# The block inversion of an RWKV-7 kernel, with its levels cut to the columns that they alter

## The chip, the cores and the metric

The kernel runs on one core of one Trainium2 chip. The metric is the device time of one execution in microseconds (us), as the median of several runs; lower is better. The engines are called as in the profile: PE is TensorE's matmul and PEld its weight load, DVE is VectorE, ACT is ScalarE, POOL is GpSimd, SP is SyncE, which issues most of the DMAs.

## The reference

One decoder block on 512 tokens of 2048 channels, in float32. A first projection feeds three things: an RWKV-7 time mixer with 16 heads of 64, sliding-window attention with 16 query heads, and two sigmoid gates that merge the two branches. After the merge follows a gated feed-forward network with a short convolution, 5632 wide. The change concerns the time mixer, whose reference is a scan over tokens with one 64 x 64 state per head:

```
def step(state, inp):
    r_t, k_t, v_t, w_t, ka_t, kb_t = inp
    sa = jnp.einsum('bhvk,bhk->bhv', state, ka_t)
    state = (state * w_t[:, :, None, :] + sa[..., None] * kb_t[:, :, None, :]
             + v_t[..., None] * k_t[:, :, None, :])
    y = jnp.einsum('bhvk,bhk->bhv', state, r_t)
    return state, y
```

Every token reads the state that the tokens before it wrote. The kernel cuts the 512 tokens into 8 chunks of 64 (NCH chunks of C). What the tokens of one chunk do to each other is a triangular system of 64 x 64 per chunk and head, and inverting its matrix replaces 64 steps by a few matrix products.

## The kernel before

**The run as a whole.** Projections come first, each a product of a 2048-channel weight slice with all 512 tokens; attention follows, then the time mixer, the merge, and the feed-forward network. A float32 product is made as three products of high and low parts: `project` (L251) issues high x high (L259), high x low (L260) and low x high (L261) for each of 16 blocks of 128 channels, each a matmul of 128 x 128 by 512 columns. So one projection tile is 48 such matmuls. `load_w` (L235) fetches the weights and makes their high part on ACT (L242) and their low part on DVE (L243).

**The time mixer.** Its 16 heads go in pairs: heads on partitions 0 to 63 and 64 to 127, eight pairs `p`. For each pair `early(p)` (L601) makes the inputs, with three projection tiles for k, r and v; `late(p)` (L656) does the chunk work; `final(p)` (L783) normalises the output, with a row of factors that goes through memory and back (L384 to L388); three gate tiles of the merge follow (`emit_gate`, L365). The loop at L805 emits late(p), early(p+1), final(p), three gates. The kernel does not fix the order of the instructions here: a planner of the framework sets each engine's order when the program is built, from estimated costs and the dependencies. On PE it puts projections of early(p+1) and of the gates between the products of late(p). Each engine then works through its instructions in that order.

**The inversion.** `BX` holds, for each of the 8 chunks, a block-diagonal 128 x 128 matrix with one 64 x 64 block per head. The inverse is built by doubling: LEVELS are 1, 2, 4, 8, 16, 32; at level m the blocks of 2m columns on the diagonal are finished from the blocks of m. The right factor of the first product, `X`, is the inverse so far, stacked for both heads (128 partitions x 8 chunks x 64 columns) and held as a high and a low f16 part, `X[:, 0]` and `X[:, 1]`. `AI` is the matrix, transposed and scaled by SG = 4096, also as two f16 parts, and `BT` the transposed inverse so far. The masks `m1` to `m32` (L103) keep of a product the columns whose place within their block of 2m is m or later, with the rows of the block's first half, and the diagonal. Level 1 is the start (L691 to L707). Each of the five other levels is (L729 to L749):

1. `mm3(ps, AI, X)`: for each of 8 chunks three f16 matmuls of 64 columns (L725 to L727), accumulated in one PSUM bank `bulk` (three banks);
2. DVE multiplies by the level's mask (L734), `split` makes the f16 parts `IW` on ACT and DVE (L205, L206);
3. `mm3(ps, BT, IW)`: 24 more matmuls;
4. ACT and DVE write the two heads' blocks of `BX` from the bank (L739, L740);
5. except in the last level, ACT and DVE write `X` anew (L742, L743), PE transposes `BX` in two times four blocks (L748), and `split` makes `BT` from them.

Then a scan over the chunks (L752 to L769) uses `BX`, and L776 to L778 make the output.

Of the kernel before, what the change touches and what calls it, by code (L numbers as in the profile page):

```python
# [8 lines left out]
F32 = mybir.dt.float32  # L9
# [3 lines left out]
AF = mybir.ActivationFunctionType  # L13
ALU = mybir.AluOpType
# [4 lines left out]
P = 128  # L19
# [3 lines left out]
C = 64  # L23
NCH = S // C
# [6 lines left out]
SG = 4096.0  # L31
# [102 lines left out]
def block_kernel(ctx: ExitStack, tc: tile.TileContext, d: Dims, a: dict, out: bass.AP):  # L134
    nc = tc.nc
    act, dve, pool, pe, sync = nc.scalar, nc.vector, nc.gpsimd, nc.tensor, nc.sync
# [31 lines left out]
    xt = [p0.tile([P, d.D], F32, name=f"xi{t}") for t in range(NT)]  # L168
# [35 lines left out]
    def split(hi, lo, src, pin=free):  # L204
        pin(act.activation(hi, src, AF.Copy))  # L205
        pin(dve.tensor_tensor(lo, src, hi.bitcast(F32) if hi.dtype == F32R else hi, op=ALU.subtract))  # L206
# [75 lines left out]
    if True:  # L282
# [109 lines left out]
        with ExitStack() as pt:  # L392
# [4 lines left out]
            def small():  # L397
                return mps.tile([P, S], F32, name="mi", tag="mi")
# [25 lines left out]
            for t in range(NKV):  # L424
# [12 lines left out]
                ps = small().rearrange("p (n c) -> p n c", c=P)  # L437
# [16 lines left out]
            for g in range(NHK):  # L454
# [7 lines left out]
                for n in range(NT):  # L462
# [9 lines left out]
                    sc = ap_.tile([P, GQ, 2 * BLK], F32, name="sc", tag="sc", bufs=2)  # L472
                    pr_ = ap_.tile([P, GQ, 2 * BLK], F32, name="pr", tag="pr", bufs=2)
                    for h in range(GQ):
                        slope = float(2.0 ** (-8.0 * (g * GQ + h + 1) / d.HQ))
                        dve.scalar_tensor_tensor(sc[:, h, k0:], K["dist"][:, k0:], slope, scp[h % 2][:, h // 2, k0:],
                                                 op0=ALU.mult, op1=ALU.add)
# [15 lines left out]
                    for kb in kbs:  # L493
                        ps = small().rearrange("p (h c) -> p h c", c=P)
# [6 lines left out]
                    ps = small()[:, : GQ * HD].rearrange("p (h c) -> p h c", c=HD)  # L501
                    for h in range(GQ):
                        for kb in kbs:
                            pe.matmul(ps[:, h], pT[:, kb, h], vt[:, n - 1 + kb, g * HD : (g + 1) * HD],  # L504
                                      start=kb == kbs[0], stop=kb == kbs[-1])
                    ot = ap_.tile([P, GQ, HD], F32, name="ot", tag="ot", bufs=2)
                    dve.tensor_tensor(ot, ps, rc.unsqueeze(2).to_broadcast([P, GQ, HD]), op=ALU.mult)
                    ps = small()[:, : GQ * HD].rearrange("p (j c) -> p j c", c=P)
# [7 lines left out]
        with ExitStack() as pr:  # L516
# [3 lines left out]
            wk = pr.enter_context(tc.tile_pool(name="wk", bufs=1, reuse_waits="tile"))  # L520
# [14 lines left out]
            def wtile(tag, bufs=1):  # L535
                return wk.tile([P, S], F32, name=tag, tag=tag, bufs=bufs)

            def bulk():
                return blk.tile([P, S], F32, name="bulk", tag="bulk")
# [15 lines left out]
            for i in range(NG):  # L555
                acc = ztile(d.c_gd + i * P)
                t = wtile("lw")
# [4 lines left out]
            def bdtile(nm):  # L562
                t = bd.tile([P, NCH, P], F32, name=nm)
                pool.memset(t[0:C, :, C:P], 0.0)
                pool.memset(t[C:P, :, 0:C], 0.0)
                return t

            BX = bdtile("BX")
# [14 lines left out]
            AI = bd.tile([P, 2, NCH, P], F16, name="AI")  # L583
            BT = bd.tile([P, 2, NCH, P], F16, name="BT")
            def r3(ap, c=C):
                return ap.rearrange("p (n c) -> p n c", c=c)
# [69 lines left out]
            def late(p, st):  # L656
# [13 lines left out]


                XIW = wk.tile([P, 4, NCH, C], F16, name="XIW", tag="rhl")
                X, IW = XIW[:, 0:2], XIW[:, 2:4]
                tt = wk.tile([P, NCH, C], F32, name="tt", tag="dd")
                HN = NCH // 2

                def mb(nm, n, h=None):
                    m = K[nm] if h is None else K[nm][h[0] : h[1]]
                    return m.unsqueeze(1).to_broadcast([m.shape[0], n, m.shape[-1]])
# [3 lines left out]
                for n0 in range(0, NCH, 2):  # L683
                    ps = bulk().rearrange("p (q c) -> p q c", c=P)
# [6 lines left out]
                for g in range(2):  # L691
                    ns = slice(g * HN, (g + 1) * HN)
                    for h, (lo, hi) in enumerate(HV):
                        own = AB[lo:hi, ns, h]
                        (dve.tensor_copy if h else act.copy)(BX[lo:hi, ns, lo:hi], own)
                        dve.tensor_tensor(tt[lo:hi, ns], own, mb("m1", HN, (lo, hi)), op=ALU.mult)
                        act.copy(own, BAR[lo:hi, ns, h, 0])
                    dve.tensor_tensor(tt[:, ns], tt[:, ns], mb("istack", HN), op=ALU.add)
                    split(X[:, 0, ns], X[:, 1, ns], tt[:, ns])
                    ps = bulk().rearrange("p (n c) -> p n c", c=P)  # L700
                    for j in range(HN):
                        pe.transpose(ps[:, j], BX[:, g * HN + j], ident)
                    at_ = wk.tile([P, HN, P], F32, name="at_", tag="at_")
                    dve.scalar_tensor_tensor(at_, ps, SG, mb("idsg", HN), op0=ALU.mult, op1=ALU.add)
                    split(AI[:, 0, ns], AI[:, 1, ns], at_)
                    for i in range(2):
                        dve.tensor_tensor(BT[:, i, ns], AI[:, i, ns], mb("t1bd", HN), op=ALU.mult)  # L707
                for g in range(2):
                    ns = slice(g * HN, (g + 1) * HN)
                    ps = bulk().rearrange("p (n c) -> p n c", c=P)  # L710
# [3 lines left out]
                    ps = bulk().rearrange("p (n h c) -> p n h c", h=2, c=C)  # L714
# [4 lines left out]
                        act.copy(SV[lo:hi, ns, 1 - h], ps[lo:hi, :, 1 - h])  # L719


                def mm3(ps, wt, xt):
                    for n in range(NCH):
                        dst = r3(ps)[:, n]
                        pe.matmul(dst, wt[:, 0, n], xt[:, 0, n], start=True, stop=False)  # L725
                        pe.matmul(dst, wt[:, 0, n], xt[:, 1, n], start=False, stop=False)
                        pe.matmul(dst, wt[:, 1, n], xt[:, 0, n], start=False, stop=True)  # L727

                for m in LEVELS[1:]:  # L729
                    last = m == LEVELS[-1]  # L730
                    ps = bulk()
                    mm3(ps, AI, X)
                    tt = wk.tile([P, NCH, C], F32, name="tt", tag="dd")
                    dve.tensor_tensor(tt, r3(ps), mb(f"m{m}", NCH), op=ALU.mult)  # L734
                    split(IW[:, 0], IW[:, 1], tt)
                    ps = bulk()
                    mm3(ps, BT, IW)
                    sc = 1.0 / (SG * SG) if last else 1.0 / SG
                    act.activation(BX[0:C, :, 0:C], r3(ps)[0:C], AF.Copy, scale=sc)  # L739
                    dve.tensor_scalar(BX[C:P, :, C:P], r3(ps)[C:P], sc, None, op0=ALU.mult)  # L740
                    if not last:
                        act.activation(X[:, 0], r3(ps), AF.Copy, scale=sc)  # L742
                        dve.scalar_tensor_tensor(X[:, 1], r3(ps), sc, X[:, 0], op0=ALU.mult, op1=ALU.subtract)  # L743
                        for g in range(2):
                            ns = slice(g * HN, (g + 1) * HN)
                            ps = bulk().rearrange("p (n c) -> p n c", c=P)
                            for j in range(HN):
                                pe.transpose(ps[:, j], BX[:, g * HN + j], ident)  # L748
                            split(BT[:, 0, ns], BT[:, 1, ns], ps)  # L749


                for n in range(NCH):  # L752
                    ps = chn.tile([P, C], F32, name="psG", tag="chn")
# [4 lines left out]
                    ps = chn.tile([P, C], F32, name="psU", tag="chn")  # L758
# [5 lines left out]
                    ps = chn.tile([P, C], F32, name="psS", tag="chn")  # L764
                    for h, (lo, hi) in enumerate(HV):
                        pe.matmul(ps[lo:hi], KK[:, n, h], UV[:, n, h], start=True, stop=True)  # L766
                    for h, (lo, hi) in enumerate(HV):
                        dve.scalar_tensor_tensor(SV[lo:hi, n + 1, h], SV[lo:hi, n, h], ee[lo:hi, n : n + 1], ps[lo:hi],
                                                 op0=ALU.mult, op1=ALU.add)  # L769


                ps = bulk()
                for n in range(NCH):
                    for h, (lo, hi) in enumerate(HV):
                        dst = r3(ps)[lo:hi, n]
# [29 lines left out]
            for p in range(NP):  # L805
                lt = late(p, st)
                if p + 1 < NP:
                    st = early(p + 1)
                final(p, lt)
                for _ in range(GATES_PER_PAIR * NK // 16):  # L810
                    emit_gate()
# [71 lines left out]
    with ExitStack() as pbb:  # L883
# [9 lines left out]
        for m, i in order:  # L893
            hi, lo, r0, n, gi = parts[i]
# [11 lines left out]
            if second:  # L906
                w = min(XC, d.D)
                for e in range(m * XC, (m + 1) * XC, w):
                    t, c0 = divmod(e, d.D)
# [309 lines left out]
    with tc.tile_pool(name="sqp", bufs=1, side="right", reuse_waits="tile") as sqp:  # L1219
# [3 lines left out]
        for i in range(len(PRODUCTS)):  # L1223
            nm = PRODUCTS[i][0]
            last = i == len(PRODUCTS) - 1
# [82 lines left out]
    with ExitStack() as pd:  # L1308
        pxy = pd.enter_context(tc.tile_pool(name="psD", bufs=1, space=PSUM, reuse_waits="tile"))
        acc = {n: banks(pxy, n) for n in "XY"}  # L1310
        for i in range(len(PRODUCTS)):
            nm = PRODUCTS[i][0]
            for c in range(NB["dn"]):
                if i == 0 and c == 1:
# [7 lines left out]
                    xa = xp.tile([P, NT, d.D], F32, name="xa")  # L1322
# [81 lines left out]
```

## Time and profile before

| | |
|---|---|
| median of 3 runs | 2936.24 us (2934.93 to 2939.33) |
| the profiled execution | 2935.18 us, of which its span is 2933.4 us |
| granted PE clock, mean | 0.997 |
| DMA, mean | 208 GB/s |
| f16 matmuls of the inversion (L725 to L727) | 1920, each with its own weight load |
| float32 transposes of BX in the levels (L748) | 256 |
| the time mixer's pairs | eight, from about 340 us to 1220 us |

The profile is one execution. A group's busy time is the sum of its instructions' durations with overlaps counted once; PE's instructions overlap, so that the mean duration of one is longer than the time from its start to the next one's start. Idle time before a group is put down to what ended it.

### The profile page before, as it was taken

The numbers are of one execution on the slowest core, as the hardware profiler recorded it, in microseconds if no ns is written. First come the engines' busy times: TensorE is split into PE (matmuls) and PEld (weight loads), VectorE is DVE, ScalarE is ACT, GpSimd is POOL, SyncE is SP. The second block draws the span as 40 slices with busy tenths as digits, with TensorE's granted clock in tenths as the row PEclk, the third lists the DMA queues.
The fourth block names the chain that finished last, engine by engine and source line by source line (L and its number), as shares of the span: only waits on it lengthen the run. The fifth ranks groups of instructions, "written<-read, shape, count | busy, mean of one in ns | idle before, by whom it ended". The sixth has DMA issues, their size and how long they took to land.

```text
span 2933.4 us, 48233 instructions
## 1 busy us (share of the span) xinstructions
PE 2879.3 (98%) x18810; PEld 2453.2 (84%) x18810; DVE 1959.2 (67%) x3250; ACT 1319.0 (45%) x2134; POOL 219.4 (7%) x288
## 2 busy tenths in 40 slices
PE   7999999999999999999999899999999999999999
PEld 6777777777777777788888899999999999888887
DVE  5565666667667666345567877777877877665555
ACT  4344434434434434232356555555555554544444
POOL 0001000000000000101000011101101010000000
PEclk9999999999999999999999999999999999999999
DMA  6865656656656656878877788888889888877785
GB/s 184 212 152 149 175 141 159 162 134 160 163 138 160 158 139 168 274 217 247 286 249 236 195 234 238 237 230 226 226 236 242 233 227 228 313 239 243 255 258 188
DMA packets 225141, 609.39 MB, mean 208 GB/s; under 512 B 24768, under 2 KB 44944, under 8 KB 223888
## 3 DMA queue, kind: packets, MB, share of 16 engines
q1 hardware_dynamic: 157504, 434.86, 46.8%
q0 software_dynamic: 36064, 132.14, 23.5%
q10 hardware_dynamic: 31344, 39.31, 3.9%
q8 instruction: 147, 2.41, 0.3%
q14 instruction: 82, 0.67, 0.1%
HBM read 556.56 MB, written 174.43 MB: 249 GB/s over the span
## 4 chain that ended last, share of the span: by engine, by line
PE 91%; DVE 3%; DMA 3%; ACT 2%; issue 1%; ACTq 0%; SPq 0%; DVEq 0%; POOLq 0%
PE X L1105 16%; PE X L972 11%; PE acc L261 11%; PE acc L260 10%; PE acc L259 10%; PE Y L972 8%; PE Y L1105 8%; PE Z L1105 4%; PE bulk L686 1%; DMA raw<-in_w_up_dram 1%; PE mi L504 1%; PE bulk L748 1%; PE psG L755 1%; PE psS L766 1%; PE bulk L725 1%
## 5 line engine op out<-in xcount | busy, mean ns | idle before, releaser
L259 PE MATMUL acc<-xhi,whi 128*128 128x512 f32 x1120 | 456.1, 407 | 5.2 <-ACT whi L242 5.2
L261 PE MATMUL acc<-xhi,wlo 128*128 128x512 f32 x1120 | 459.4, 410 | 1.7 <-DVE wlo L243 1.7
L260 PE MATMUL acc<-xlo,whi 128*128 128x512 f32 x1120 | 452.7, 404 | 0.0
L242 ACT ACTIVATE whi<-raw 128x512 fp32r<-128x512 f32 x352 | 220.1, 629 | 478.0 <-PE acc L260 368.5
L965 DVE TENSOR_TENSOR wlo<-raw,whi 128x1024 fp32r<-128x1024 f32 x210 | 257.1, 1225 | 203.6 <-ACT whi L964 201.9
L243 DVE TENSOR_TENSOR wlo<-raw,whi 128x512 fp32r<-128x512 f32 x352 | 239.8, 688 | 198.9 <-ACT whi L242 191.2
L964 ACT ACTIVATE whi<-raw 128x1024 fp32r<-128x1024 f32 x210 | 222.6, 1060 | 289.1 <-PE X L972 150.6
L1105 PE MATMUL X<-b,whi 128*128 128x256 f32 x1472 | 269.2, 283 | 2.3 <-DVE u L1125 0.9
L1105 PE MATMUL X<-t,whi 128*128 128x256 f32 x1408 | 259.8, 285 | 10.1 <-DVE u L1125 9.6
L1088 DVE TENSOR_TENSOR wlo<-raw,whi 128x1024 fp32r<-128x1024 f32 x176 | 215.0, 1223 | 77.0 <-ACT whi L1087 76.9
L1105 PE MATMUL Y<-t,whi 128*128 128x256 f32 x1408 | 257.2, 283 | 0.0
L259 PEld LDWEIGHTS acc<-xhi,whi 128*128 128x128 f32 x1120 | 211.3, 189 | 44.8 <-ACT whi L242 6.4
L261 PEld LDWEIGHTS acc<-xhi,wlo 128*128 128x128 f32 x1120 | 211.0, 188 | 44.9 <-DVE wlo L243 4.4
L260 PEld LDWEIGHTS acc<-xlo,whi 128*128 128x128 f32 x1120 | 211.0, 188 | 40.4 <-issue 1.6
L1087 ACT ACTIVATE whi<-a 128x1024 fp32r<-128x1024 f32 x132 | 139.4, 1056 | 216.6 <-DVE a L1081 214.7
L1105 PEld LDWEIGHTS X<-b,whi 128*128 128x128 f32 x1472 | 229.5, 192 | 3.1 <-issue 2.4
L1105 PEld LDWEIGHTS X<-t,whi 128*128 128x128 f32 x1408 | 221.7, 194 | 10.7 <-DVE u L1125 7.1
L1105 PEld LDWEIGHTS Y<-t,whi 128*128 128x128 f32 x1408 | 219.6, 192 | 0.0
L1105 PE MATMUL X<-b,wlo 128*128 128x256 f32 x736 | 208.5, 283 | 2.3 <-DVE wlo L1088 2.3
L1088 DVE TENSOR_TENSOR wlo<-a,whi 128x1024 fp32r<-128x1024 f32 x132 | 161.7, 1225 | 67.4 <-ACT whi L1087 66.7
L1105 PE MATMUL X<-t,wlo 128*128 128x256 f32 x704 | 200.4, 285 | 0.2 <-DVE wlo L1088 0.2
L1105 PE MATMUL Y<-t,wlo 128*128 128x256 f32 x704 | 199.2, 283 | 0.0
(347 smaller groups left out, 6117.7 us busy)
## 6 DMA issues: line engine op xcount, KB each, us to landing
raw<-in_w_up_dram SPq DMA_DIRECT2D x180, 512.0 KB
raw<-in_w_z_dram SPq DMA_DIRECT2D x288, 256.0 KB
s_dn<-in_w_dn_dram POOLq DMA_DIRECT2D x88, 512.0 KB, 6.7
raw<-in_w_up_dram POOLq DMA_DIRECT2D x88, 512.0 KB, 8.6
raw<-s_dn SPq DMA_DIRECT2D x88, 512.0 KB
raw<-in_w_dn_dram SPq DMA_DIRECT2D x66, 512.0 KB
a<-in_w_up_dram SPq DMA_DIRECT2D x48, 512.0 KB
s_dn<-in_w_dn_dram SPq DMA_DIRECT2D x44, 512.0 KB
```

The source lines that it names most:

```text
L242: pin(act.activation(hi, raw, AF.Copy))
L243: pin(dve.tensor_tensor(lo, raw, hi.bitcast(F32), op=ALU.subtract))
L259: pe.matmul(acc, whi[:, j], xhi[:, k], start=first, stop=False)
L260: pe.matmul(acc, whi[:, j], xlo[:, k], start=False, stop=False)
L261: pe.matmul(acc, wlo[:, j], xhi[:, k], start=False, stop=last)
L504: pe.matmul(ps[:, h], pT[:, kb, h], vt[:, n - 1 + kb, g * HD : (g + 1) * HD], start=kb == kbs[0], stop=kb == kbs[-1])
L964: act.activation(whi, wr, AF.Copy)
L965: dve.tensor_tensor(wlo, wr, whi.bitcast(F32), op=ALU.subtract)
L972: pe.matmul(dst, l[:, q, ts], r[:, es], start=fst and j == 0, stop=lst and j == 2, skip_group_check=True)
L1087: pin(act.activation(hi, t, AF.Copy))
L1088: pin(dve.tensor_tensor(lo, t, hi.bitcast(F32), op=ALU.subtract))
L1105: pin(pe.matmul(ps, l[:, k], r[:, k], start=start and k + i == 0, stop=last and i == 2, skip_group_check=True))
```

## The change

A level's mask keeps only half of the columns, those whose place within a block of 2m is m or later; the others of X and BX stay as they were. The changed kernel makes the products for these 32 of 64 columns alone:

- `mm3` issues two matmuls per chunk in place of three. The first has the left factor's high part and, as its 64 columns, the altered columns of the right factor's high part beside those of its low part; the second has the left factor's low part and the 32 altered columns of the high part, accumulated onto the first half of the same columns.
- The two halves of the bank are then summed: ACT copies the second half to SBUF, DVE adds the first half to it in place, into a tile `half_` with the tag of `tt`. The mask and the split work on this sum, 256 elements per partition in place of 512.
- `IW` lies with high and low parts of a chunk next to each other. The altered columns of `X` are read where they are, in runs of m with gaps of m.
- BX and X are written in their altered columns only, from the sum in SBUF. So BX must hold the start too: two more writes per half of the chunks (ACT and DVE). BX is now at the scale of the inverse in every level, and the factor SG comes back when BT is made from its transposes, on ACT by the scale of the copy and on DVE by a `scalar_tensor_tensor` in place of the subtraction in `split`.

The number of weight loads goes with that of the matmuls, from 24 to 16 per product. The transposes stay.

```
-                X, IW = XIW[:, 0:2], XIW[:, 2:4]
+                X = XIW[:, 0:2]
+                CH = C // 2
+                IW = XIW[:, 2].rearrange("p n (e c) -> p n e c", e=2)
...
                     split(AI[:, 0, ns], AI[:, 1, ns], at_)
+                    act.activation(BX[0:C, ns, 0:C], tt[0:C, ns], AF.Copy, scale=1.0 / SG)
+                    dve.tensor_scalar(BX[C:P, ns, C:P], tt[C:P, ns], 1.0 / SG, None, op0=ALU.mult)
...
-                def mm3(ps, wt, xt):
+                def mm3(wt, both, high):
+                    ps = bulk()
+                    p4 = ps.rearrange("p (n e c) -> p n e c", n=NCH, e=2)
                     for n in range(NCH):
-                        dst = r3(ps)[:, n]
-                        pe.matmul(dst, wt[:, 0, n], xt[:, 0, n], start=True, stop=False)
-                        pe.matmul(dst, wt[:, 0, n], xt[:, 1, n], start=False, stop=False)
-                        pe.matmul(dst, wt[:, 1, n], xt[:, 0, n], start=False, stop=True)
+                        pe.matmul(ps[:, n * C : (n + 1) * C], wt[:, 0, n], both(n), start=True, stop=True)
+                        pe.matmul(p4[:, n, 0], wt[:, 1, n], high(n), start=False, stop=True, skip_group_check=True)
+                    t = wk.tile([P, NCH, C], F32, name="half_", tag="dd")[:, :, :CH]
+                    act.activation(t, p4[:, :, 1], AF.Copy)
+                    dve.tensor_tensor(t, t, p4[:, :, 0], op=ALU.add)
+                    return t
...
                 for m in LEVELS[1:]:
                     last = m == LEVELS[-1]
-                    ps = bulk()
-                    mm3(ps, AI, X)
-                    tt = wk.tile([P, NCH, C], F32, name="tt", tag="dd")
-                    dve.tensor_tensor(tt, r3(ps), mb(f"m{m}", NCH), op=ALU.mult)
-                    split(IW[:, 0], IW[:, 1], tt)
-                    ps = bulk()
-                    mm3(ps, BT, IW)
-                    sc = 1.0 / (SG * SG) if last else 1.0 / SG
-                    act.activation(BX[0:C, :, 0:C], r3(ps)[0:C], AF.Copy, scale=sc)
-                    dve.tensor_scalar(BX[C:P, :, C:P], r3(ps)[C:P], sc, None, op0=ALU.mult)
+                    def altered(x):
+                        return x.rearrange("p n (b a m) -> p n b a m", a=2, m=m)[:, :, :, 1]
+                    def by_block(x):
+                        return x.rearrange("p n (b m) -> p n b m", m=m)
+                    xa = X.rearrange("p e n (b a m) -> p e n b a m", a=2, m=m)[:, :, :, :, 1]
+                    t = mm3(AI, lambda n: xa[:, :, n], lambda n: xa[:, 0, n])
+                    dve.tensor_tensor(by_block(t), by_block(t), altered(mb(f"m{m}", NCH)), op=ALU.mult)
+                    split(IW[:, :, 0], IW[:, :, 1], t)
+                    t = mm3(BT, lambda n: IW[:, n].rearrange("p e c -> p (e c)"), lambda n: IW[:, n, 0])
+                    act.activation(altered(BX[0:C, :, 0:C]), by_block(t[0:C]), AF.Copy, scale=1.0 / (SG * SG))
+                    dve.tensor_scalar(altered(BX[C:P, :, C:P]), by_block(t[C:P]), 1.0 / (SG * SG), None, op0=ALU.mult)
                     if not last:
-                        act.activation(X[:, 0], r3(ps), AF.Copy, scale=sc)
-                        dve.scalar_tensor_tensor(X[:, 1], r3(ps), sc, X[:, 0], op0=ALU.mult, op1=ALU.subtract)
+                        act.activation(xa[:, 0], by_block(t), AF.Copy, scale=1.0 / SG)
+                        dve.scalar_tensor_tensor(xa[:, 1], by_block(t), 1.0 / SG, xa[:, 0], op0=ALU.mult, op1=ALU.subtract)
                         for g in range(2):
...
-                            split(BT[:, 0, ns], BT[:, 1, ns], ps)
+                            act.activation(BT[:, 0, ns], ps, AF.Copy, scale=SG)
+                            dve.scalar_tensor_tensor(BT[:, 1, ns], ps, SG, BT[:, 0, ns], op0=ALU.mult, op1=ALU.subtract)
```

## The prediction

> **What bounds the kernel now.** I read the page first, for the engine that carries the span and for the chain that ended last, then the stretches of the stage that the diff touches, then groups by line and the order of PE's instructions in one level.
>
> ```profile
> span 2933.4 us, 48233 instructions
> PE 2879.3 (98%) x18810; PEld 2453.2 (84%) x18810; DVE 1959.2 (67%) x3250; ACT 1319.0 (45%) x2134; POOL 219.4 (7%) x288
> PE 91%; DVE 3%; DMA 3%; ACT 2%; issue 1%; ACTq 0%; SPq 0%; DVEq 0%; POOLq 0%
> ```
>
> PE is busy for 98% of the span and holds 91% of the chain. An average says little about one stage, so the next view gives one period (one of the eight head pairs) and its pieces: busy time and instructions of PE, PEld, DVE, ACT and POOL, then the granted clock, the DMA share and GB/s.
>
> ```profile
> 566.50:572.00 5.50, 5.48 (x45) 4.36 (x43) 5.43 (x12) 4.96 (x13) 0.81 (x1) 1.00 1.04 226
> 572.00:609.00 37.00, 36.66 (x370) 28.44 (x368) 26.39 (x43) 20.92 (x39) 1.61 (x2) 1.00 0.59 138
> 609.00:645.00 36.00, 36.00 (x222) 23.99 (x221) 24.90 (x67) 10.24 (x24) 2.41 (x3) 1.00 0.50 113
> 645.00:670.00 25.00, 24.86 (x110) 19.28 (x109) 12.55 (x30) 6.09 (x12) 1.41 (x2) 1.00 0.72 188
> 566.50:675.50 109.00, 108.50 (x767) 80.67 (x766) 74.22 (x164) 44.82 (x91) 7.10 (x10) 1.00 0.63 154
> ```
>
> A period is 109.00 us, and PE works in 108.50 of them, at a granted clock of 1.00. The inversion's five levels are the second row, the scan over chunks the third; in the fourth PE does little but gate projections. PE is full in all four, since projections (L259 to L261) fill what the inversion leaves. So PE time taken out of the inversion shortens the period, as long as the projections still cover the inversion's own waits.
>
> **What goes from PE.** The products of the inversion are the f16 matmuls:
>
> ```profile
> L725 PE MATMUL bulk<-XIW,BT 128*128 128x64 f16 x320 | 36.5, 193 | 0.7
> L725 PE MATMUL bulk<-XIW,AI 128*128 128x64 f16 x320 | 34.3, 194 | 1.8 <-ACT AI L205 1.8
> L726 PEld LDWEIGHTS <-BT 128*128 128x128 f16 x320 | 27.9, 98 | 11.0 <-issue 11.0
> ```
>
> L726 and L727 have as many again: 6 x 320 = 1920 matmuls in 80 products (8 pairs, 5 levels, 2 each) of 24. Their mean of about 193 ns is a latency and not a price, for they overlap. The price is the step from start to start, which the order in time shows (start, duration, instruction); here is one product with X between its first and last matmul, and the first of the next level:
>
> ```profile
> 580.75 0.20 PE L725 MATMUL bulk<-XIW,AI 128*128 128x64 f16 x1
> ...
> 581.43 0.19 PE L727 MATMUL bulk<-XIW,AI 128*128 128x64 f16 x1
> 581.46 0.47 PE L260 MATMUL acc<-xlo,whi 128*128 128x512 f32 x1
> ...
> 587.86 0.20 PE L725 MATMUL bulk<-XIW,AI 128*128 128x64 f16 x1
> ```
>
> 24 matmuls in 581.46 - 580.75 = 0.71 us: 29.6 ns each. The change issues 16 a product: eight with high and low parts side by side (2 x 32 = 64 columns, as wide as today's) and eight 32 columns wide. The first eight cost 29.6 ns each by this row. No row shows a f16 matmul of 32 columns. By its columns alone it would take half, 14.8 ns; if loading its weights sets the step, still 29.6. The row that tells between these is that of the narrowest matmuls there are, against a run of wide ones:
>
> ```profile
> 579.40 1.03 PE L748 MATMUL bulk<-ident,BX 128*128 128x128 f32 x8
> 580.19 0.48 PE L261 MATMUL acc<-xhi,wlo 128*128 128x512 f32 x1
> ...
> 610.41 1.05 PE L377 MATMUL bulk<-cst,lg 128*128 128x2 f32 x8
> 611.33 0.49 PE L261 MATMUL acc<-xhi,wlo 128*128 128x512 f32 x1
> ```
>
> Eight transposes of 128 columns take 0.79 us, eight matmuls of 2 columns 0.92 us: fewer columns bought nothing there. So I take 29.6 ns for all sixteen and keep 14.8 for the range. What goes is then the count: 80 x 8 = 640 matmuls x 29.6 ns = **18.9 us**.
>
> [...]
>
> A second gain: today the first matmul of a product with IW needs only the high part, and the order lets it go ahead alone:
>
> ```profile
> 576.21 0.20 PE L725 MATMUL bulk<-XIW,BT 128*128 128x64 f16 x1
> 576.25 0.48 PE L260 MATMUL acc<-xlo,whi 128*128 128x512 f32 x1
> 576.56 0.40 PE L261 MATMUL acc<-xhi,wlo 128*128 128x512 f32 x1
> 576.80 0.40 PE L259 MATMUL acc<-xhi,whi 128*128 128x512 f32 x1
> 577.03 0.20 PE L726 MATMUL bulk<-XIW,BT 128*128 128x64 f16 x1
> ```
>
> The lone matmul takes 0.04 us to the next start, and the projection behind it 0.31 where its neighbours step by 0.23 to 0.24, so the switch costs 0.04 + 0.31 - 0.23 - 0.03 = 0.09 us. The PEld row above has 11.0 us of idle before L726's loads; what L726 waited for, us and times, is one line:
>
> ```profile
>   issue: 11.0, 40
> ```
>
> 40 times, once for each product with IW. In the change the first matmul needs both parts, nothing can go ahead, and 40 x 0.09 = **3.6 us** go. If the order still splits them, this term is nothing.
>
> **What is added beside PE.** Per level, in the order in which it runs; the rows are the operations that go and the nearest to those that come:
>
> ```profile
> L734 DVE TENSOR_TENSOR tt<-bulk,cst 128x512 f32<-128x512 f32 x40 | 27.3, 682 | 0.0
> L205 ACT ACTIVATE XIW<-tt 128x512 f16<-128x512 f32 x40 | 25.0, 625 | 33.5 <-DVE tt L734 33.5
> L206 DVE TENSOR_TENSOR XIW<-tt,XIW 128x512 f16<-128x512 f32 x40 | 27.6, 689 | 12.7 <-ACT XIW L205 12.6
> L739 ACT ACTIVATE BX<-bulk 64x512 f32<-64x512 f32 x40 | 23.6, 591 | 58.7 <-PE bulk L727 58.7
> L740 DVE TENSOR_SCALAR BX<-bulk 64x512 f32<-64x512 f32 x40 | 27.8, 695 | 50.3 <-ACT BX L739 50.0
> L742 ACT ACTIVATE XIW<-bulk 128x512 f16<-128x512 f32 x32 | 19.0, 595 | 10.7 <-DVE BX L740 10.0
> L743 DVE SCALAR_TENSOR_TENSOR XIW<-bulk,XIW 128x512 f16<-128x512 f32 x32 | 22.1, 690 | 11.5 <-ACT XIW L742 11.3
> ...
> L1121 ACT ACTIVATE u<-X 128x256 f32<-128x256 f32 x172 | 64.5, 375 | 89.0 <-PE X L1105 86.4
> L1125 DVE TENSOR_TENSOR u<-u,Y 128x256 f32<-128x256 f32 x44 | 18.4, 417 | 1.8 <-PE Y L1105 0.8
> L205 ACT ACTIVATE XIW<-tt 128x256 f16<-128x256 f32 x16 | 6.6, 415 | 0.2
> L206 DVE TENSOR_TENSOR XIW<-tt,XIW 128x256 f16<-128x256 f32 x16 | 6.7, 418 | 0.5 <-ACT XIW L205 0.3
> L695 ACT COPY BX<-AB 64x256 f32<-64x256 f32 x16 | 6.5, 405 | 14.0 <-DVE AB L689 14.0
> L695 DVE COPY BX<-AB 64x256 f32<-64x256 f32 x16 | 4.7, 291 | 0.2
> ```
>
> Each product gains an ACT copy of half the bank (256 elements, as L1121: 0.375 us) and a DVE sum (as L1125: 0.417), and what follows runs on 256 elements in place of 512: mask 0.682 to about 0.417, high 0.625 to 0.415, low 0.689 to 0.418, BX 0.591 to 0.405 on ACT and 0.695 to about 0.291 on DVE, X 0.595 to about 0.415 and 0.690 to about 0.418. Before the levels each half of the chunks gains one more write of BX on ACT (0.405) and on DVE (0.291).
> DVE per pair: 10 x 0.417 - 5 x 0.265 - 5 x 0.271 - 5 x 0.404 - 4 x 0.272 + 2 x 0.291 = about -1.0 us of 74.2. ACT: 10 x 0.375 - 5 x 0.210 - 5 x 0.186 - 4 x 0.180 + 2 x 0.405 = +1.9 us of 44.8. Neither comes near 109.
>
> In the chain of one level the parts were 0.71 us and about 0.19 of the last matmul's end for each product, then 0.682 + 0.625 + 0.689, and 0.591 + 0.695 + 0.595 + 0.690 (ACT and DVE take the bank in turn: L740 waits for L739, L742 for L740): 6.37 us of the 587.86 - 580.75 = 7.11 measured; 0.74 over eight hand-overs, 0.09 each. After: products of 16 x 0.03 + 0.19 = 0.66; 0.375 + 0.417 + 0.417 + 0.415 + 0.418; 0.66 again; 0.375 + 0.417 + 0.405 + 0.415 + 0.418: 5.39 us, and ten hand-overs at 0.09 make 6.3. If L740 still follows L739 and X waits for it, 6.7. The level's chain grows no longer.
>
> So the added work costs **nothing** in the sum: projections hide it. Cover there is: 110 instructions of PE run in 645 to 670, where the next pair's first products could begin as soon as the gates leave PE. Without it, three hand-overs more per level, 0.09 each, would be 40 x 0.27 = 11 us. The two writes of BX ahead of the levels fall in 566.5 to 572, where DVE is busy for 5.43 of 5.50 us: they push the first level back by 0.6 us at most, under the same cover (8 x 0.6 = 4.8 us without it).
> What is late next is the end of a pair, whose normalisation waits for a row from memory:
>
> ```profile
> 663.39 0.69 DVE L796 TENSOR_TENSOR yc<-yc,rsb 128x512 f32<-128x512 f32 x1 [5.98 <-DMA rsb<-rsd]
> ...
> 671.10 0.42 DVE L689 TENSOR_TENSOR AB<-bulk,cst 128x256 f32<-128x256 f32 x1
> ```
>
> The next pair's L689 starts 7.7 us behind it, and I take 22.5 / 8 = 2.8 us out of each period: the wait stays off the path. The buffers do not change: three bulk banks, of which a product now frees its own after the sum.
>
> **The sum**: -18.9 - 3.6 = -22.5 us on the profiled execution, which took 2935.18 us (its span of 2933.4 and 1.8 around it): 2912.7. The median of the runs lies 1.06 us above that execution, so about **2914 us**, 0.8% faster.
>
> **The rivals.**
> *Half the columns, half the step.* At 14.8 ns for the 640 narrow matmuls the gain grows by 9.5 us: **2904**. For it: a projection of 512 columns does step 0.23 us, so long streams go by columns. Against it: the 2-column rows.
> *Strided reading.* At level m the product with X reads runs of m elements with gaps of m. No row has such a read. If a read paid for the whole stretch that it spans, the 640 matmuls with X would take 2 x 29.6 ns: +18.9 us, which leaves 3.6 us of gain, **2932**. At no extra cost it is the forecast. The nearest rows read without gaps, so I take none. [...]
> *Products late for their places (slower).* PE works in a fixed order, with a set number of projections ahead of each product. Each product now waits behind two more operations on ACT and DVE, in shapes with gaps. If the order was laid for a shorter chain than runs, PE stands at the product's first weights, with the projections queued behind it. The gain is 22.5 / 80 = 0.28 us a product, so a mean delay above that decides; at 0.45 us, what a single 256-element operation takes, it is 36 - 22.5 = +13.5 us: **2950**. Against it: PE's idle before L725 is 0.7 + 1.8 us over 80 products today, 0.03 each.
> *No effect.* The order of the whole stage is laid out anew and loses elsewhere what the products gain, by some 0.28 us a product: **2936**.
>
> **How the numbers follow.** Forecast 0.60, half the step 0.12, strided reading 0.08, late products 0.12, no effect 0.08. Runs of this kernel spread by some 0.15%, so 0.2%, 5.9 us, is about the least difference that can be told. Forecast and half the step are faster by more: 0.72. Strided reading and no effect lie within: 0.16. Late products: 0.12. The range runs from 2902, just under half the step, to 2937, just over no effect, and leaves out the late products and the tails.
>
> **What would show it.** In the profile after: 1280 f16 matmuls, 640 of them 32 columns wide, in unbroken runs of 16 that last about 0.47 us (0.36 by columns alone; twice that with X if gaps cost); a period near 106.2 us with PE still full; some 176 instructions on DVE and 103 on ACT per period. Were PE idle before the first weights of a product by over 0.1 us each, the hiding would be wrong; were the steps right and the period still 109 us, PE would not be what sets it.

## The result and the profile after

The changed kernel takes 2912.07 us (median of 4 runs, 2911.18 to 2912.88) against 2935.59 us for the kernel before (median of 4): a ratio of 0.9916, 95% interval 0.9904 to 0.9929. That is 23.5 us less; 2914 us was forecast. The profiled execution took 2912.28 us, 22.9 us less than the one before.

The page of the changed kernel, its span, busy times and the chain by engine:

```profile
span 2910.5 us, 47181 instructions
PE 2857.5 (98%) x18170; PEld 2441.0 (84%) x18170; DVE 1951.6 (67%) x3346; ACT 1330.6 (46%) x2230; POOL 220.0 (8%) x288
PE 93%; DMA 3%; DVE 2%; ACT 2%; issue 1%; ACTq 0%; SPq 0%; DVEq 0%; POOLq 0%
```

PE has lost 640 instructions and is as full as before. Three periods of the changed kernel, cut at the first product (L688) of each pair; busy time and instructions of PE, PEld, DVE, ACT and POOL, granted clock, DMA share, GB/s:

```profile
448.96:554.80 105.84, 105.53 (x687) 78.88 (x686) 73.58 (x175) 46.45 (x103) 7.34 (x10) 1.00 0.60 154
554.80:660.51 105.71, 105.38 (x688) 78.88 (x687) 73.52 (x175) 46.46 (x103) 7.06 (x9) 1.00 0.63 158
977.83:1083.57 105.74, 105.45 (x687) 78.88 (x686) 73.55 (x175) 46.42 (x103) 7.07 (x9) 1.00 0.61 155
```

A period is 105.7 us in place of 109.0, with 80 PE instructions fewer, and DVE and ACT where the prediction put them. The groups of f16 matmuls, and the order in time of one product with X in the third level:

```profile
L730 PE MATMUL bulk<-XIW,AI 128*128 128x64 f16 x320 | 24.3, 190 | 0.5
L731 PE MATMUL bulk<-XIW,AI 128*128 128x32 f16 x320 | 23.6, 178 | 0.0
L730 PE MATMUL bulk<-XIW,BT 128*128 128x64 f16 x320 | 23.0, 190 | 0.5
L731 PE MATMUL bulk<-XIW,BT 128*128 128x32 f16 x320 | 22.4, 177 | 0.0
```

```profile
581.55 0.19 PE L730 MATMUL bulk<-XIW,AI 128*128 128x64 f16 x1
581.57 0.18 PE L731 MATMUL bulk<-XIW,AI 128*128 128x32 f16 x1
...
581.96 0.18 PE L731 MATMUL bulk<-XIW,AI 128*128 128x32 f16 x1
581.98 0.48 PE L261 MATMUL acc<-xhi,wlo 128*128 128x512 f32 x1
```

Sixteen matmuls in an unbroken run, 581.98 - 581.55 = 0.43 us, where 24 took 0.71.

**Where the 22.9 us are.** Five periods of each trace (the third to the seventh), with the time from each start on PE to the next put down to the earlier instruction, give per period:

| us per period | before | after |
|---|---|---|
| the period | 109.04 | 105.75 |
| f16 matmuls (240, then 160) | 7.30 | 4.51 |
| projections (288) | 74.90 | 74.32 |
| other matmuls and transposes | 26.84 | 26.92 |
| switches from f16 to a projection (a number, not a time) | 15 | 10 |
| from a level's product with X to the next level's (mean of all eight pairs) | 7.92 | 7.50 |

The mean time from one f16 matmul's start to the next start, by line, was 29.8 to 31.0 ns before; after, it is 29.8 for the 64 columns and 26.5 for the 32.
The eighth pair starts 22.3 us earlier, and behind its start only 0.6 us more are gained, though its products shrank like the others'. What took it back stands around the last gates, in the view of waits (who waited for whom: us, times, longest) from 1190 to 1250 us, of before and then of after:

```profile
ACT whi L242 <- DMA raw<-in_w_z_dram: 24.7, 6, 8.2
...
PE acc L259 <- ACT whi L242: 5.2, 3, 2.3
```

```profile
DVE wlo L243 <- ACT whi L242: 30.4, 11, 6.8
...
ACT whi L242 <- DMA raw<-in_w_z_dram: 25.5, 8, 6.8
...
PE acc L259 <- ACT whi L242: 7.2, 3, 3.9
```

Behind the last pair no scan is left to run beside the gates, and their weights come late: PE stands 7.2 us in place of 5.2. Behind the longest of these waits the granted clock was 0.50 from 1225.19 to 1228.60 us, where the kernel before kept 1.00 from 1190 to 1250.

### The profile page after: what moved, and what is told of

Read it like the earlier page. It is cut to its first block, busy times and chain, and to the rows that moved or that the text cites. A ratio compares the mean times of both kernels' runs of the same rounds, so it can differ in the third digit from the quotient of the medians.

```text
span 2910.5 us, 47181 instructions
## 1 busy us (share of the span) xinstructions
PE 2857.5 (98%) x18170; PEld 2441.0 (84%) x18170; DVE 1951.6 (67%) x3346; ACT 1330.6 (46%) x2230; POOL 220.0 (8%) x288
## 4 chain that ended last, share of the span: by engine, by line
PE 93%; DMA 3%; DVE 2%; ACT 2%; issue 1%; ACTq 0%; SPq 0%; DVEq 0%; POOLq 0%
PE X L1118 17%; PE X L985 11%; PE acc L261 11%; PE acc L259 11%; PE acc L260 11%; PE Y L985 8%; PE Y L1118 8%; PE Z L1118 4%; DMA raw<-in_w_z_dram 1%; PE bulk L760 1%; PE bulk L730 1%; PE bulk L688 1%; PE psG L768 1%; PE mi L504 1%; PE psS L779 1%; PE bulk L599 1%
```

## The experiments

The theory after the result: PE sets the period, so the count of matmuls and the switches pay, and the added work is hidden. The rival: what pays is the shorter chain of work on half as many elements. All ratios are against the kernel before, run on the same chip beside them; in the diffs `-` is the changed kernel, in the third and the fourth the kernel before. Levels and periods are worked out from the traces as in the table.

### Width: the second matmul 64 columns wide

```
-    pe.matmul(p4[:, n, 0], wt[:, 1, n], high(n), start=False, stop=True, skip_group_check=True)
+    pe.matmul(ps[:, n * C : (n + 1) * C], wt[:, 1, n], both(n), start=False, stop=True, skip_group_check=True)
```

> The changed kernel with its second matmul made 64 columns wide again (low part of the left factor times high and low part of the right; the product low x low is added, which the kernel leaves out otherwise). Theory (the gain is the count of matmuls, the width buys little): the 640 matmuls step 29.8 ns in place of the 26.5 that the changed kernel's trace shows, 640 x 3.3 = 2.1 us, about 2914 us. Rival (narrow matmuls are what pays): most of the 23 us goes, above 2925 us.

Measured: 2910.46 us, ratio 0.9912 (0.9898 to 0.9925): not slower. The step did grow, from 26.5 to 29.2 ns, and the f16 matmuls from 4.51 to 4.79 us a period, 2.2 us in all as the theory says; but the period was 104.9 us, for the planner laid the rest out otherwise: the projections cost 73.86 us in place of 74.32, the other matmuls 26.25 in place of 26.92. So narrowness is worth 2 us of PE time, and an order laid anew scatters by more: here 1.6 us less time with 2.2 us more work.

### Half the columns without side by side

```
-    pe.matmul(ps[:, n * C : (n + 1) * C], wt[:, 0, n], both(n), start=True, stop=True)
-    pe.matmul(p4[:, n, 0], wt[:, 1, n], high(n), start=False, stop=True, skip_group_check=True)
...
+    dst = p4[:, n, 0]
+    pe.matmul(dst, wt[:, 0, n], high(n), start=True, stop=False)
+    pe.matmul(dst, wt[:, 0, n], low(n), start=False, stop=False)
+    pe.matmul(dst, wt[:, 1, n], high(n), start=False, stop=True)
...
-    act.activation(t, p4[:, :, 1], AF.Copy)
-    dve.tensor_tensor(t, t, p4[:, :, 0], op=ALU.add)
```

> Half the columns, but not side by side: three matmuls of 32 columns per chunk, accumulated, and no sum of two halves behind them. Theory: PE pays for 24 matmuls of about 26.5 ns per product in place of 16 that take 28.1 in the mean; 80 x (0.636 - 0.450) = 15 us more than the changed kernel, so about 2927 us, and still 8 us under the kernel before (24 x 29.6 ns, and the lone first matmul may be back). The ACT copy and the DVE sum that are gone give nothing. Rival (the gain is the shorter chain of work on half as many elements on ACT and DVE): as fast as the changed kernel or faster, 2912 or less.

Measured: 2916.97 us, ratio 0.9935 (0.9922 to 0.9947), 5 us above the changed kernel, not 15. The matmuls cost what the theory says (6.27 us a period, 1.76 more than in the changed kernel), but the level is 6.51 us in place of 7.50, and the other matmuls, most of them the scan's, cost 25.22 us in place of 26.92. Neither account is whole: of the 14 us of f16 time, 9 come back elsewhere, and this run does not tell whether by the two operations of the sum that are gone or by the new order.

### Side by side without half the columns

```
-    pe.matmul(dst, wt[:, 0, n], xt[:, 0, n], start=True, stop=False)
-    pe.matmul(dst, wt[:, 0, n], xt[:, 1, n], start=False, stop=False)
-    pe.matmul(dst, wt[:, 1, n], xt[:, 0, n], start=False, stop=True)
+    pe.matmul(p4[:, j].rearrange("p e c -> p (e c)"), wt[:, 0, n], xt[:, :, n], start=True, stop=True)
+    pe.matmul(p4[:, j, 0], wt[:, 1, n], xt[:, 0, n], start=False, stop=True, skip_group_check=True)
...
+    act.activation(t[:, ns], p4[:, :, 1], AF.Copy)
+    dve.tensor_tensor(t[:, ns], t[:, ns], p4[:, :, 0], op=ALU.add)
```

> High and low parts side by side, but all 64 columns: per chunk one matmul of 128 columns and one of 64, over two banks, with sum, mask and splits on 512 elements as before. Theory (16 matmuls, but the step of a wide one is set by its columns): 128 columns take about twice 29.6 - 3 ns, near 56 ns, so a product costs 8 x (56 + 29.6) = 0.69 us against 0.71 before; 80 x 0.02 and the lone switches give about 5 us: 2930 to 2932 us. Rival (the number of matmuls alone is what pays): as the changed kernel, 2912 to 2914 us.

Measured: 2954.37 us, ratio 1.0056 (1.0043 to 1.0070): slower than before. The step of 128 columns is 57.4 ns and the f16 matmuls cost 6.96 us a period, as expected (the 3 ns taken off the doubled step were the author's estimate, which no run had shown; 2 x 29.8 - 57.4 = 2.2 ns came out); the number of matmuls alone does not pay. But the level grew to 9.66 us, and PE stands at the next pair's first products (L686, waits of PE between 400 and 1200 us):

```profile
PE bulk L686 <- DVE yc L804: 16.4, 7, 3.8
```

So a longer chain is not hidden here: neither theory nor rival had that price.

### The lone first matmul

```
-    pe.matmul(dst, wt[:, 0, n], xt[:, 0, n], start=True, stop=False)
-    pe.matmul(dst, wt[:, 0, n], xt[:, 1, n], start=False, stop=False)
+    pe.matmul(dst, wt[:, 0, n], xt[:, 1, n], start=True, stop=False)
+    pe.matmul(dst, wt[:, 0, n], xt[:, 0, n], start=False, stop=False)
```

> The kernel before with the first two matmuls of each chunk exchanged: high x low first, then high x high, so that the first matmul of a product waits for the low part and cannot go ahead of the others. Nothing else is changed. Theory: 40 switches of 0.09 us go, 3.6 us, ratio about 0.9988, and the trace has no lone matmul. Rival (the lone matmul costs nothing, PE would have stood otherwise): ratio 1.000.

Measured: 2933.43 us, ratio 0.9994 (0.9985 to 1.0003), undecided between 0.9988 and 1. The trace decides more: no lone matmul is left, and the switches from f16 to projections fell from 15 to 10 a period and from 1.32 to 0.89 us, the expected 0.09 each. But PE's waits ahead of the products grew by as much, from 0.67 to 1.19 us. In the order in time:

```profile
582.41 0.39 PE L260 MATMUL acc<-xlo,whi 128*128 128x512 f32 x1
582.94 0.19 PE L725 MATMUL bulk<-XIW,BT 128*128 128x64 f16 x1
```

0.53 us from the projection to the product, where a projection's step is 0.23: the product stands where it stood, and now waits there for the low part. In this trace the term is worth nothing by itself, though the ratio's interval does not exclude it; in the changed kernel the waits did not grow (0.61 us), and the 0.43 us a period are real there.

### The price of the chain: two and six operations more

```
     dve.tensor_tensor(t, t, p4[:, :, 0], op=ALU.add)
+    for _ in range(1):
+        act.activation(t, t, AF.Copy)
+        dve.tensor_tensor(t, t, K["ones"][:, 0:CH].unsqueeze(1).to_broadcast([P, NCH, CH]), op=ALU.mult)
```

That is the kernel with two operations more; the one with six has `range(3)`.

> The changed kernel with two more operations in the chain of each product, behind the sum: an ACT copy of it onto itself and a DVE product with ones, 256 elements each. The result is unchanged. They lengthen the chain of a pair by 10 products x (0.41 + 0.42 + two hand-overs of 0.09) = about 10 us. Theory (projections hide what lies beside PE): within 2 us of the changed kernel, 2911 to 2915 us. Rival (the chain sets the period, and the change won by keeping it short): 8 x 10 = 80 us more, near 2990 us.

> The same with three such pairs of operations in each product: about 30 us of chain more per pair of heads. Theory: the cover in a period is the stretch in which PE does little but gate projections, some 20 to 25 us; what goes over it, 5 to 10 us a period, is paid, so 2950 to 2995 us. If the planner finds more cover, nothing is paid. Rival (the chain sets the period): 8 x 30 = 240 us more, near 3150 us.

Measured: 2960.15 us (ratio 1.0077, 1.0064 to 1.0091) and 3049.73 us (1.0384, 1.0368 to 1.0400). Both lie between what theory and rival said. The level grew by 2.4 and by 6.0 us, so the chain of a pair by 12 and by 30; a period grew by 6.1 and by 21. With two operations 6 of the 12 us were paid (at a granted clock of 0.98), where a cover of 20 to 25 us would have hidden them all. With six the price of the chain can't be read off: 23 more projections run in a period there, 5 us that in the changed kernel stand behind the eighth pair's start, and the granted clock of the five periods is 0.90. With two operations, the place is the start of the next pair (DVE and ACT in the order in time, then PE):

```profile
668.33 0.58 ACT L371 ACTIVATE gt<-acc 128x512 f32<-128x512 f32 x1
...
678.69 0.69 DVE L812 TENSOR_TENSOR yc<-yc,rsb 128x512 f32<-128x512 f32 x1 [3.90 <-DMA rsb<-rsd]
679.41 0.42 DVE L698 TENSOR_TENSOR tt<-AB,cst 64x256 f32<-64x256 f32 x1
...
684.16 0.96 PE L704 MATMUL bulk<-ident,BX 128*128 128x128 f32 x4 [4.36 <-ACT whi L242]
```

The last gate's result is written at 668.33, and the row of factors has come from memory only at 678.69; the next pair's mask (L698) stands behind it in DVE's queue, and PE has nothing left.

### No sum, with the count kept

The matmuls of the changed kernel with the rest of the three-matmul kernel, so that the part in the bank's second half is left out of the result:

```
-    act.activation(t, p4[:, :, 1], AF.Copy)
-    dve.tensor_tensor(t, t, p4[:, :, 0], op=ALU.add)
-    return t
+    return p4[:, :, 0]
```

> The changed kernel without the sum of the two halves: the same 16 matmuls per product, but mask, BX and X are taken from the first half of the bank alone, straight from PSUM (the product of the left factor's high part and the right factor's low part is computed and left out). Its chain is that of the kernel with three accumulating matmuls (a level of about 6.5 us against 7.5), its PE work that of the changed kernel. Theory now (a shorter chain leaves projections for the scan, where PE otherwise waits between small products; a us of level is worth about 1.7 us of a period of 105.7): a period near 104.0 us, about 2899 us. Rival (projections hide the two operations entirely, as the prediction had it, and the three-matmul kernel came as low by luck of its order): a period of 105.7 us, 2910 to 2914 us.

Measured: 2906.31 us, ratio 0.9903 (0.9889 to 0.9916), a period of 105.0 us: between the two. Against the three-matmul kernel, whose level is the same (6.52 and 6.51 us), 24 to 16 matmuls are worth 10.7 us, of 14.1 us less of f16 time, and the two intervals do not overlap: PE's count pays. Against the changed kernel, the two operations of the sum, 5 us of chain a pair, would cost 5.8 us in all. That is not shown: these intervals overlap, and the order alone moved the first experiment by some 4 us.

### One operation more, and where the cover ends

```
     dve.tensor_tensor(t, t, p4[:, :, 0], op=ALU.add)
+    dve.tensor_tensor(t, t, K["ones"][:, 0:CH].unsqueeze(1).to_broadcast([P, NCH, CH]), op=ALU.mult)
```

> The changed kernel with one more DVE product with ones behind each sum, 256 elements: 0.42 us and a hand-over, 10 times a pair, some 5 us of chain per pair, half of what the kernel with two more operations added. Theory now (there is no point below which the chain is free; each us of level costs PE some time in the scan, and behind about 6 us per pair the row of factors from memory comes late besides): a period 1 to 2 us longer, 2920 to 2930 us. Rival (hidden until the cover runs out, which took more than 10 us): 2910 to 2914 us.

Measured: 2947.50 us, ratio 1.0043 (1.0029 to 1.0056), worse than either said: 5.3 us more of chain a pair, 4.8 us more of period. The trace shows one place (PE in the order in time, then DVE):

```profile
667.87 1.89 PE L688 MATMUL bulk<-BAR,BKK 128*128 128x256 f32 x8
672.36 1.13 PE L688 MATMUL bulk<-BAR,BKK 128*128 128x256 f32 x4 [2.60 <-DVE yc L815]
```

```profile
669.10 0.69 DVE L810 TENSOR_TENSOR yc<-yc,rsb 128x512 f32<-128x512 f32 x1 [5.34 <-DMA rsb<-rsd]
...
671.61 0.69 DVE L815 TENSOR_TENSOR yc<-yc,bulk 128x512 f32<-128x512 f32 x1
```

The normalisation of the pair holds one of the three banks until its row has come and L815 has read the bank; the next pair's third pair of products needs that bank. Two kernels put the last product of the normalisation, which L815 reads, in a bank of the scan's pool: the one with the operation more and the changed kernel itself.

```
-    ps = bulk()
+    ps = chn.tile([P, S], F32, name="gps", tag="chn")
     lora(ps, ag, 1, 1 + NG)
```

> The kernel with one more DVE operation behind each sum, and the product of the gate's low-rank factors in the pair's normalisation (final) in a bank of the scan's pool in place of one of the three that the next pair's first products use. In the kernel without this, PE stood 2.6 us per pair at those products (and about 1.2 more behind it) until the row of factors had come from memory and the bank was read. Theory (the edge of the cover is this bank, held until the row has come): the stall goes, 3 to 4 us of each of 7 periods, 2918 to 2926 us. Rival (the chain itself sets the period once it is 5 us longer, whatever the bank): 2944 us or more.

> The changed kernel with the same move of a bank and nothing else. There the row arrives 6 us before the next pair's first products, and no stall is seen there. Theory: no effect beyond the order's own scatter, 2908 to 2916 us. Rival (the bank binds the order even there): a period 1 us shorter or more, under 2905 us.

Measured with the operation more: 2925.15 us, ratio 0.9968 (0.9956 to 0.9979), 22 us less for one bank, as the theory said; a period is 107.7 us, and PE's wait for yc is gone. So the first edge of the cover is shown. The other 13 us of the operation's price stay, and another wait now stands at the same products (waits of PE between 400 and 1200 us):

```profile
PE bulk L688 <- DVE MM L692: 8.5, 4, 4.0
```

In the changed kernel alone: 2908.37 us, ratio 0.9905 (0.9891 to 0.9920), within what was expected; it has the lowest median of the kernels that compute the whole, but its interval and the changed kernel's overlap.

### Gates moved out of the tail

```
-    for _ in range(GATES_PER_PAIR * NK // 16):
+    for _ in range(GATES_PER_PAIR * NK // 16 + (p < 4)):
```

> The changed kernel with four gate tiles in place of three behind each of the first four pairs, so that four in place of eight are left behind the last pair, where PE now waits 7.2 us for weights that come late from memory. Theory (there the transfers are the bound, at a DMA share above 1.0): with fewer gate weights to fetch there, part of these 7.2 us goes, 2906 to 2911 us. Rival: the gates there were cover for the loads of the merge, and the wait comes back behind other weights, 2912 us or more.

Measured: 2916.74 us, ratio 0.9934 (0.9920 to 0.9948): 4.7 us worse, as the rival has it. The idle time of PE behind the last pair stayed, at some 7 us as in the changed kernel, but at other weights.

## Why the prediction was right, step by step

**PE sets the period**: right. PE is busy for 105.45 of 105.74 us, and the period fell with its work.

**The count, 18.9 us**: right in kind and short in size. The f16 matmuls cost 7.30 - 4.51 = 2.79 us a period less, 22.3 us over eight pairs. Of this 640 x 30.4 ns (their mean before) = 19.5 us is the count, 2.5 us the narrow matmuls, which step 26.5 ns and not 30.4, and the rest the wide ones. The choice of the upper end for the unknown width was nearly right, and half the step is refuted: 26.5 and not 14.8 ns, and wider matmuls made the kernel no slower. The row of 2 columns gave the direction and not the size: its eight instructions are four float32 products (L377 stands 208 times in the trace, for 104 products), at about 0.11 us an instruction, and none of them is f16.

**The lone matmul, 3.6 us**: the size was right (0.43 us a period, 3.4 in all), the reason incomplete: taken alone, the switch it saves came back as a wait for the low part. In the changed kernel it did not; that the product's place in PE's order moved there too is the likely reason, and no run isolates it.

**The added work at nothing**: right as far as can be told, but with less to spare than was said. The changed kernel without the sum is 5.8 us faster, about what an order's scatter can do. The level's chain did not grow, as was said, since the same change shortened its other operations: it went from 7.92 to 7.50 us, and without the sum to 6.5. But one operation more in each product cost 35 us, so projections hide far less beside PE than the prediction had it. The estimate of 6.3 to 6.7 us missed a queue. In the changed kernel DVE and ACT run:

```profile
574.25 1.29 DVE L762 SCALAR_TENSOR_TENSOR BT<-bulk,BT 128x512 f16<-128x512 f32 x2 [0.63 <-ACT BT L761]
575.45 0.41 DVE L734 TENSOR_TENSOR half__5774<-half__5774,bulk 128x256 f32<-128x256 f32 x1
```

```profile
574.59 0.39 ACT L733 ACTIVATE half__5774<-bulk 128x256 f32<-128x256 f32 x1
```

The copy of the product's second half ends at 574.98, and the sum starts at 575.45: BT's low parts stand ahead of it on DVE, as they do in all 32 levels that follow another, for 0.47 us or more. That is about half of the 0.8 us that the estimate's upper end lacks; the rest was not traced to a place.

**The cover, the gates from 645 to 670 us**: wrong by size, and its edge was misplaced. It was said that the row from memory is what comes next and stays off the path; it does in the changed kernel, but one operation more per product brought it onto the path at once. The bank that the row holds back was not seen.

**The rivals.** Half the step: refuted. Strided reading: the f16 matmuls with X take 2.30 us a period and those with IW, which lie without gaps, 2.20; one product with X a pair is issued in two pieces, and nothing near a doubling is there. Late products: in the changed kernel refuted (PE's waits before products 0.61 us a period against 0.67), but the mechanism is real and near, as the kernel with one operation more shows, at another place than forecast. No effect: refuted.

**What was not foreseen**: the eighth pair's share, some 2.7 us, was given back at the late gate weights, where PE waited 2.0 us longer and then ran 3.4 us at half the clock. The f16 matmuls and the switches together would have given 22.3 + 3.4 = 25.7 us; 22.9 came out. That 22.5 was said is in part luck: one term too small and one loss not seen.

## What to carry to other kernels

A PE that was busy for 99.5% of a period here still took a gain in PE's work at nearly full value (22.9 of 25.7 us), but the cover over the other engines' chain is a number of its own: find the first thing that the next round needs from the last one (here a bank held until a row came back from memory) and measure the time to it, for beyond it the chain is paid, here 4.8 of the first 5.3 us. Small f16 matmuls were paid nearly by the piece up to 64 columns (26.5 ns at 32, 29.8 at 64, 57.4 at 128); making them narrower bought 3 ns each, making them fewer 30. Any edit also lays the order anew, which alone moved a time here by some 4 us, so a smaller difference between two kernels says nothing about their operations. Where a change removes one wait from an in-order queue, look at what the next instruction in it waits for: in the trace with the first two matmuls exchanged, the switch saved came back as a wait.

## What was not expected of the hardware

One stall was paid twice here: behind the longest wait for the last gates' weights, of 3.9 us, the changed kernel's granted clock fell to 0.50 for 3.4 us (busy times by engine, then the clock):

```profile
1217.70:1247.70 30.00, 26.08 (x108) 20.83 (x107) 12.87 (x21) 11.63 (x21) 1.62 (x2) 0.94 0.72 210
```

The mean clock of these 30 us is 0.94. Not every wait did this: behind one of 2.3 us at 1205 us in the same trace the clock stayed at 1.00. With six operations more in each product, where PE stood often, it is 0.962 over the whole span. And a projection that follows an f16 matmul costs 0.09 us over its plain step of 0.23, one that follows a matmul of another kind 0.11 us (both counted where another projection comes next), in the kernel before as in the changed one; the changed kernel has 10 and 34 of them in a period, 0.9 + 3.6 = 4.5 of its 105.7 us.
